# A blocked causal convolution: H1's sums stored in reverse, one F operation for H0, a second output pair split over three engines, and new orders

## The chip, the cores and the metric

One core of one Trainium2 chip. The metric is the device time of one launch in microseconds (us), lower is better.

## The reference

A causal convolution along the sequence with full matrices as taps: each output row is the sum over eight taps of an earlier input row times a 512 x 512 matrix.

```python
B, S, D, K = 8, 4096, 512, 8
out = np.zeros_like(x)                       # x: (B, S, D) float32
for k in range(K):                           # kernel: (K, D, D) float32
    shifted = x moved k rows down, zeros ahead
    out += np.matmul(shifted, kernel[k])
```

## The kernel before

**Tiling.** The 8 x 4096 rows are cut into 128 runs of 256 consecutive rows, one run per partition. A product is a 128 x 512 by 512 x 512 matrix product in bf16 (4 matmuls of 128 x 512, accumulated in PSUM): it applies one matrix to one row position of all 128 runs. The input is loaded with a cast to bf16 into DRAM buffers `xd` (GpSimd's queue), four rows at a time, and transposed from there into `XR`, a ring of 20 row positions (SyncE's queue).

**Fewer products.** The first 4 rows of each run are computed directly (`direct(tap, t)`, 32 products). The other 252 are done in 21 blocks of 12 rows. A block has four nodes, in this order: PL, MI, H1, H0. A node takes sums and differences of input rows and of the eight weight matrices (the weight sums `wsum` and `plus` are made once, on VectorE) and needs 9 products. Nodes 3 and 4, of the first block, are "leaf" nodes: they take 11 products and fewer sums. The outputs are put together from the four nodes' results.

**Names.** `do(name, k)` runs one step of node k; an order is a list of tokens `name.i`, where i counts from the block's PL node (0 PL, 1 MI, 2 H1, 3 H0, 4 and up the next block's). The steps of a node:
- VectorE: `z` (row differences or sums from XR into Z), `s` (sums of Z rows two apart, into S), `A` (two sums of neighbouring Z rows), `F0` and `F1` (two sums each of neighbouring S rows, into F). All are bf16 with both inputs in SBUF. `d0` and `d1` make the first half of a PSUM pair from the second and DT.
- TensorE: `a1`, `a0`, `u` (three products into the bank pair q), `v0`, `v1` (from S), `l00`, `l01`, `l10`, `l11` (from F).
- ScalarE: a copy inside q behind a1; `s0`, `s1` (seeds of the result pairs p[0], p[1]), `dt` (DT).
- `e0`, `e1` take the result pairs out of PSUM: PL's on ScalarE (into cc, two passes), MI's on VectorE (into dd), H1's and H0's on VectorE into y buffers, with a store. H0's writes dd in place.
- `ga0`, `gb0`, `ga1`, `gb1`: the two halves of the middle outputs, cc and dd added on GpSimd, with a store. `E0` (ScalarE copies the second half of H1's first pair) and `ya0` (GpSimd adds dd to it) split H1's first pair.
- `r0`, `r1`, `r2`: GpSimd issues the load of four rows three blocks ahead; `x12`, `x16`, `x20`: SyncE issues a transpose.

In H0 four of the five s rows are computed, the fifth is H1's, which lies in S already; F0 of H0 reads it by a broadcast.

**What sets the order.** The schedule is manual: each engine runs its instructions in the order in which the program emits them, and waits only for the data and the buffers. `ORDER` is run once per block; ahead of it stands a long hand-written start for the first two blocks. S, F, Z and DT exist once, so the next node's step waits until the last reader of the old contents is through. Output tiles come from a pool of 5 buffers (`ypool`), handed out in the order in which they were released. `behind(i)` adds a wait: a GpSimd operation or load starts only after the VectorE operation emitted last. In the last block ga1 has no such wait.

Of the kernel before, what the change touches and what calls it, by code (L numbers as in the profile page):

```python
# [14 lines left out]
def kernel(  # L15
# [244 lines left out]
    def node_e(n, b_):  # L260
        p, t = n.p[b_], n.t + 2 * b_
        first = n.k <= 4
        if n.a == PL:
            cc[b_] = y_tile()
            if first:
                nc.scalar.mul(out=cc[b_], in_=p, mul=0.5)
            else:
                nc.scalar.copy(out=cc[b_], in_=p)  # L268
                dd[b_] = y_tile()
                nc.scalar.mul(out=dd[b_], in_=cc[b_], mul=-0.5)  # L270
        elif n.a == MI:
            if first:
                dd[b_] = y_tile()
                stt(dd[b_], p, -0.5, cc[b_], ADD)
            else:
                stt(dd[b_], p, 0.5, dd[b_], ADD)
        elif n.a == H1:
            yy[b_] = yy.get(b_) or y_tile()
            if first or b_ == HI:
# [4 lines left out]
        elif n.k == len(nodes) - 1 and b_ == HI:
            for j, eng in ((HI, nc.scalar), (LO, nc.sync)):
                stt(dd[b_][:, j], dd[b_][:, j], -1.0, p[:, j], SUB)
                eng.dma_start(out=orr[:, t + 8 + j, :], in_=dd[b_][:, j])
        else:
            if first:
                tt(dd[b_], dd[b_], p, SUB)  # L290
            else:
                stt(dd[b_], dd[b_], -1.0, p, SUB)
# [2 lines left out]
    def node_E(n):
        if n.a == H1 and n.k > 4:
            yy[LO] = yy.get(LO) or y_tile()
            nc.scalar.copy(out=yy[LO][:, 1], in_=n.p[LO][:, 1])

    def node_y(n):  # L300
        if n.a == H1 and n.k > 4:
            y = yy.pop(LO)
            behind(nc.gpsimd.tensor_tensor(out=y[:, 1], in0=y[:, 1], in1=dd[LO][:, 1], op=SUB))
            store(n.t, y)
# [4 lines left out]

    def middle_half(n, b_, j):  # L310
        behind(nc.gpsimd.tensor_tensor(out=cc[b_][:, j], in0=cc[b_][:, j], in1=dd[b_][:, j], op=ADD), b_ > j and n.k)  # L311
# [132 lines left out]
    nc.vector.memset(zero, 0.0)
    nc.sync.dma_start(out=XF, in_=xr[:, 0:4, :])
    cast(nc.vector.tensor_copy, 2, 4)
    make_identity(nc, ident)
    for k in range(7):
        fill(pair(2 + k % 2))
    rows(H[:, 4:8], RUN - 4, 4)  # L450
    cast(nc.scalar.copy, 0, 2)
    transpose_pe("x0", 2, xin[0], 0, 4)
    load_w(0)
    load_w(4)
    fill(pair(3))
    fill(pair(3))
    here(nc.scalar.copy, 0, "x0", 0, 2)
    transpose_pe("h4", 3, H, 4, 8)
    here(nc.scalar.copy, 0, "x0", 2, 4)
    fill(pair(2))  # L460
    history(nc.scalar.copy, -4, "h4")
    direct(0, 1)
    go(3, "v0")
    go(2, "d1")
    direct(0, 0)
    direct(0, 2)
    direct(0, 3)
    direct(4, 2)
    fill(pair(2))
    load_w(1)  # L470
    direct(4, 0)
    direct(1, 1)
    direct(1, 3)
    wsum(MI, HI, HI)
    load_w(5)
    load_w(3)
    wsum(MI, HI, LO)
# [89 lines left out]
    node_a1(nodes[2])
    go(1, "s")
    node_v(nodes[1], 1)
    direct_out(1)  # L570
    go(1, "l01")
    go(1, "l00")
    node_d(nodes[1], 1)
    go(1, "e0")
    go(1, "u")
    go(1, "a0")
    transpose_x(12)
    go(1, "l10")
    go(1, "z")
    do("x16", 1)  # L580
    go(1, "l11")
    go(1, "s1")
    wsum(H1, MID, MID)
    go(1, "s0")
    go(1, "v0")
    go(1, "dt")
    go(1, "F0")
    go(1, "A")
    go(1, "d0")
    go(1, "a1")  # L590
    go(2, "F1")
    go(1, "v1")
    go(2, "l01")
    go(2, "l00")
# [108 lines left out]
```

## Time and profile before

| | |
|---|---|
| time, median of 3 runs | 718.18 us (717.39 to 718.66) |
| the profiled execution | span 717.2 us, 8960 instructions; its device time isn't listed apart from the runs, the lowest of which is 717.39 us |
| TensorE matmuls | 696.0 us busy (97%), 3205 instructions |
| VectorE | 683.3 us (95%), 767 |
| ScalarE | 287.7 us (40%), 448 |
| GpSimd | 167.5 us (23%), 180 |
| granted TensorE clock | 0.998 |
| DMA | 138.86 MB, mean 194 GB/s |

An engine's busy time says nothing of when it was needed: matmuls are pipelined, and the record of one (0.38 us) overlaps the next. Lines of the profile name the line, the engine, the operation, its output and input by the program's names (pp: PSUM pairs, y: output buffers, w: weights, WX and the early S and A), the sizes and a count. VectorE is DVE, ScalarE ACT, GpSimd POOL, SyncE SP. All two-input operations of VectorE are emitted by `tt` (L84) or `stt` (L87), so the output's name and size tell which step a row is. Consecutive rows of the same kind are merged, with their count behind the x.

### The profile page before, as it was taken

The page shows a single profiled execution, that of the slowest core. Times are in us where ns is not written, and L with a number is a line of the kernel's source. Part 1 is how long each engine was busy: PE and PEld are TensorE (multiplying, and loading weights), DVE is VectorE, ACT ScalarE, POOL GpSimd, SP SyncE. Part 2 cuts the span into 40 slices and gives each one's busy share as a digit, 9 for nine tenths or more (in the row PEclk, how much of TensorE's full clock was granted, in tenths as well). Part 3 has the DMA queues.
Part 4 walks back from the last instruction along what each step waited for, and adds up shares of the span by engine and source line. Part 5 has one row for each costly group of instructions (what it writes and reads, how often), then busy time and mean ns, then how long its engine had stood idle before and what let it go on. Part 6 is the DMA issues. An engine that isn't in the chain of part 4 may idle for free.

```text
span 717.2 us, 8960 instructions
## 1 busy us (share of the span) xinstructions
PE 696.0 (97%) x3205; PEld 315.0 (44%) x3270; DVE 683.3 (95%) x767; ACT 287.7 (40%) x448; POOL 167.5 (23%) x180
## 2 busy tenths in 40 slices
PE   7989999999999999999999999999999999999995
PEld 3444444444444444444444444444444444444442
DVE  1899999999999999999999999999999999999994
ACT  3043244343435444343443434353443434444341
POOL 4200012213131221304122131312213041221212
PEclk9999999999999999999999999999999999999999
DMA  9996988788797878879788887977788698855414
GB/s 194 209 225 139 235 156 243 158 233 181 206 226 174 233 167 231 181 189 217 182 241 158 231 184 205 229 176 229 168 237 174 189 224 178 238 119 186 157 68 175
DMA packets 159515, 138.86 MB, mean 194 GB/s; under 512 B 130160, under 2 KB 134256, under 8 KB 159344
## 3 DMA queue, kind: packets, MB, share of 16 engines
q1 hardware_dynamic: 145312, 99.37, 46.6%
q0 software_dynamic: 13728, 38.15, 31.6%
q10 hardware_dynamic: 432, 0.79, 0.3%
q8 instruction: 25, 0.41, 0.2%
q14 instruction: 18, 0.15, 0.1%
HBM read 77.33 MB, written 99.09 MB: 246 GB/s over the span
## 4 chain that ended last, share of the span: by engine, by line
PE 84%; DVE 5%; issue 5%; DMA 0%; POOL 0%; DVEq 0%; POOLq 0%
PE pp L127 84%; DVE w L84 2%; DVE Z L84 2%; DVE y L87 1%; DVE S L84 1%; DMA out_dram<-y 0%; POOL y L311 0%; DVE y L84 0%; DVE F L84 0%; DVE pp L87 0%; DVE pp L84 0%; POOL xd L93 0%; DVEq L84 0%; DVEq L87 0%; POOLq L93 0%
## 5 line engine op out<-in xcount | busy, mean ns | idle before, releaser
L127 PE MATMUL pp<-w,F 128*128 128x512 bf16 x1285 | 310.4, 379 | 3.2 <-DVE pp L87 1.3
L127 PE MATMUL pp<-w,Z 128*128 128x512 bf16 x941 | 231.9, 379 | 2.7 <-DVE Z L84 1.7
L127 PEld LDWEIGHTS <-F 128*128 128x128 bf16 x1312 | 128.3, 98 | 157.6 <-issue 3.4
L311 POOL TENSOR_TENSOR y<-y 128x512 f32<-128x512 f32 x80 | 101.7, 1272 | 406.0 <-DVE F L84 266.1
L127 PE MATMUL pp<-w,S 128*128 128x512 bf16 x658 | 157.5, 379 | 0.7
L84 DVE TENSOR_TENSOR Z<-XR 128x2048 bf16<-128x2048 bf16 (+3 forms) x109 | 154.5, 1435 | 2.5
L127 PEld LDWEIGHTS <-Z 128*128 128x128 bf16 x960 | 92.3, 98 | 118.2 <-DVE Z L84 9.4
L198 ACT COPY pp<-pp 128x512 f32<-128x512 f32 x82 | 46.7, 570 | 221.1 <-PE pp L127 221.1
L84 DVE TENSOR_TENSOR S<-Z 128x2560 bf16<-128x2560 bf16 (+1 forms) x81 | 114.5, 1413 | 0.0
L84 DVE TENSOR_TENSOR F<-S 128x1024 bf16<-128x1024 bf16 x160 | 111.1, 694 | 1.9 <-PE pp L127 1.9
L127 PEld LDWEIGHTS <-S 128*128 128x128 bf16 x672 | 65.8, 98 | 79.4 <-issue 0.2
L214 ACT COPY pp<-pp 128x512 f32<-128x512 f32 (+1 forms) x84 | 48.9, 582 | 76.5 <-PE pp L127 76.5
L93 POOL DMA_DIRECT2D xd<-in_x_dram x61 | 32.7, 536 | 103.7 <-DVE F L84 48.6
L84 DVE TENSOR_TENSOR pp<-DT,pp 128x512 f32<-128x512 f32 x82 | 56.3, 687 | 0.2 <-PE pp L127 0.2
L87 DVE SCALAR_TENSOR_TENSOR pp<-pp,DT 128x512 f32<-128x512 f32 x82 | 56.5, 689 | 0.0
L216 ACT ACTIVATE pp<-pp 128x512 f32<-128x512 f32 (+1 forms) x84 | 50.1, 596 | 15.2 <-PE pp L127 9.8
L84 DVE TENSOR_TENSOR Z<-Z 128x1024 bf16<-128x1024 bf16 x78 | 53.4, 684 | 0.7
L87 DVE SCALAR_TENSOR_TENSOR y<-pp,y 128x1024 f32<-128x1024 f32 x42 | 51.0, 1215 | 0.0
L220 ACT COPY DT<-pp 128x512 f32<-128x512 f32 x82 | 48.9, 597 | 2.6 <-PE pp L127 2.6
L268 ACT COPY y<-pp 128x1024 f32<-128x1024 f32 x40 | 40.6, 1016 | 22.9 <-PE pp L127 21.7
L87 DVE SCALAR_TENSOR_TENSOR y<-y,pp 128x1024 f32<-128x1024 f32 (+1 forms) x41 | 48.3, 1181 | 0.3 <-PE pp L127 0.3
L270 ACT ACTIVATE y<-y 128x1024 f32<-128x1024 f32 x40 | 42.3, 1057 | 2.8 <-DMA out_dram<-y 0.6
(35 smaller groups left out, 248.5 us busy)
## 6 DMA issues: line engine op xcount, KB each, us to landing
out_dram<-y SPq DMA_DIRECT2D x126, 512.0 KB, 4.2
xd<-in_x_dram POOLq DMA_DIRECT2D x61, 512.0 KB, 5.6
w<-in_kernel_dram POOLq DMA_DIRECT2D x8, 512.0 KB, 16.8
w<-in_x_dram SPq DMA_DIRECT2D x1, 1024.0 KB, 4.8
w<-in_x_dram POOLq DMA_DIRECT2D x2, 512.0 KB, 14.0
XR<-xd SPq DMA_TRANSPOSE x61, 4.8
out_dram<-y ACTq DMA_DIRECT2D x3, 256.0 KB, 3.4
w<-in_x_dram POOLq DMA_DIRECT2D x2, 256.0 KB, 18.1
```

The lines of the kernel that those rows point to most:

```text
L84: last["dve"] = nc.vector.tensor_tensor(out=o, in0=a, in1=b, op=op)
L87: last["dve"] = nc.vector.scalar_tensor_tensor(out=o, in0=a, scalar=by, in1=b, op0=MUL, op1=op)
L93: return nc.gpsimd.dma_start(out=o, in_=src)
L127: nc.tensor.matmul(bank, lhsT=comp[:, c * P:(c + 1) * P], rhs=w[:, c, :], start=start and c == 0, stop=c == DC - 1, skip_group_check=True)
L198: nc.scalar.copy(out=n.q[:, 0], in_=n.q[:, 1])
L214: nc.scalar.copy(out=o, in_=q)
L216: nc.scalar.mul(out=o, in_=q, mul=-1.0)
L220: nc.scalar.copy(out=DT, in_=n.q[:, 0])
L268: nc.scalar.copy(out=cc[b_], in_=p)
L270: nc.scalar.mul(out=dd[b_], in_=cc[b_], mul=-0.5)
L311: behind(nc.gpsimd.tensor_tensor(out=cc[b_][:, j], in0=cc[b_][:, j], in1=dd[b_][:, j], op=ADD), b_ > j and n.k)
```

## The change

H1's five s rows are written to S in reverse, so the row that H0 takes over from it is row 0, and H0's four F sums become one operation over rows 0 to 4 (`F.3`). H1's second pair is split like its first: VectorE takes the first half, ScalarE copies the second (`E1`), GpSimd adds dd (`ya1`). The signs and scales of cc and dd change: PL's e is one pass on ScalarE, `m0` and `m1` double cc later, H0's e is a plain subtraction. Tap 0's weights are loaded in four parts (`q0` to `q3`), and its 16 matmuls are issued part by part (`P0` to `P3`). The first cast and the first copies are shared differently between VectorE and ScalarE, the identity is made behind the first loads. ORDER is new, and the start is a token list, `SETUP`, that reaches into the third block.

```diff
-            tt(n.s[:, 0:4], n.z[:, n.o + 1:n.o + 5], n.z[:, n.o + 3:n.o + 7], ADD)
+            tt(n.s[:, 1:5], z[:, o + 1:o + 5], z[:, o + 3:o + 7], ADD)
+        elif n.rev:
+            tt(n.s[:, ::-1], z[:, o:o + 5], z[:, o + 2:o + 7], ADD)
...
-        if not n.shares:
-            tt(f, s[:, 2 * b_:2 * b_ + 2], s[:, 2 * b_ + 1:2 * b_ + 3], ADD)
-        elif b_ == LO:
-            tt(f, s[:, 0:1].to_broadcast([P, 2, D]), s[:, 1:5:3], ADD)
-        else:
-            tt(f, s[:, 1:3], s[:, 2:4], ADD)
+        n.whole = b_ is None
+        a, b = (0, 4) if n.whole else (2 * b_, 2 * b_ + 2)
+        i = 2 - a if n.rev and not n.whole else a
+        tt(F[:, a:b], n.s[:, i:i + b - a], n.s[:, i + 1:i + 1 + b - a], ADD)
...
-            if first:
-                nc.scalar.mul(out=cc[b_], in_=p, mul=0.5)
-            else:
-                nc.scalar.copy(out=cc[b_], in_=p)
-                dd[b_] = y_tile()
-                nc.scalar.mul(out=dd[b_], in_=cc[b_], mul=-0.5)
+            nc.scalar.mul(out=cc[b_], in_=p, mul=0.5)
         elif n.a == MI:
-            if first:
-                dd[b_] = y_tile()
-                stt(dd[b_], p, -0.5, cc[b_], ADD)
-            else:
-                stt(dd[b_], p, 0.5, dd[b_], ADD)
+            dd[b_] = y_tile()
+            stt(dd[b_], p, -0.5, cc[b_], ADD)
         elif n.a == H1:
             yy[b_] = yy.get(b_) or y_tile()
-            if first or b_ == HI:
-                tt(yy[b_], p, dd[b_], ADD if first else SUB)
+            if b_ in SPLIT:
+                tt(yy[b_][:, 0], p[:, 0], dd[b_][:, 0], ADD)
+            else:
+                tt(yy[b_], p, dd[b_], ADD)
                 store(t, yy.pop(b_))
...
+            tt(dd[b_], dd[b_], p, SUB)
             store(t + 8, dd[b_])
...
+    def node_E(n, b_):
+        yy[b_] = yy.get(b_) or y_tile()
+        nc.scalar.copy(out=yy[b_][:, 1], in_=n.p[b_][:, 1])
+
+    def node_y(n, b_):
+        y = yy.pop(b_)
+        behind(nc.gpsimd.tensor_tensor(out=y[:, 1], in0=y[:, 1], in1=dd[b_][:, 1], op=ADD))
+        store(n.t + 2 * b_, y)
+
+    def twice(n, b_):
+        nc.scalar.mul(out=cc[b_], in_=cc[b_], mul=2.0)
...
+    def direct_part(c):
+        w = W[(K - 1) >> 2, (K - 1) >> 1 & 1, (K - 1) & 1]
+        for t in range(HEAD):
+            nc.tensor.matmul(pd[t // 2][:, t % 2], lhsT=XR[:, place(t), c * P:(c + 1) * P], rhs=w[:, c, :],
+                             start=c == 0, stop=c == DC - 1, skip_group_check=True)
...
     ORDER = """
-        d1.1 l01.1 l00.1 s.2 a0.2 x12.0 u.2 l10.1 e1.0 s0.2 e0.1 s1.2 l11.1 v0.2 z.3 F0.2 A.3 F1.2 ga0.2
-        v1.2 x20.1 dt.2 a1.3 d0.2 r0.2 l01.2 e1.1 l00.2 s.3 a0.3 u.3 gb0.2 d1.2 e0.2 l10.2 E0.2 z.4 F0.3
-        r1.2 A.4 l11.2 s1.3 F1.3 s0.3 v0.3 v1.3 ya0.2 r2.2 dt.3 d0.3 a1.4 l01.3 e1.2 l00.3 s.4 gb1.2 a0.4
-        d1.3 e0.3 u.4 l11.3 z.5 s0.4 F0.4 A.5 s1.4 dt.4 ga1.2 v0.4 v1.4 l10.3 d0.4 a1.5 d1.4 l00.4 l01.4
-        a0.5 u.5 e0.4 F1.4 e1.3 s.5 s0.5 l10.4 dt.5 s1.5 z.6 A.6 x16.4 l11.4 F0.5 v0.5 v1.5 a1.6 d0.5 F1.5
+        d1.1 l01.1 l00.1 e1.0 a0.2 u.2 s.2 s0.2 l10.1 l11.1 e0.1 m0.1 v0.2 z.3 s1.2 F0.2 v1.2 dt.2 r0.2
+        ga0.2 A.3 e1.1 d0.2 a1.3 l01.2 x12.0 gb0.2 l00.2 F1.2 x20.1 m1.1 d1.2 a0.3 s.3 u.3 e0.2 z.4 l10.2
+        s0.3 l11.2 E0.2 v0.3 r1.2 A.4 F.3 s1.3 dt.3 ya0.2 a1.4 d0.3 v1.3 l01.3 l00.3 e1.2 a0.4 s.4 gb1.2 u.4
+        d1.3 e0.3 z.5 F0.4 E1.2 dt.4 ya1.2 l11.3 s0.4 r2.2 ga1.2 l10.3 v0.4 A.5 s1.4 v1.4 a1.5 d0.4 l00.4
+        l01.4 d1.4 F1.4 a0.5 e0.4 u.5 e1.3 s.5 z.6 l10.4 dt.5 s0.5 x16.4 F0.5 l11.4 v0.5 A.6 d0.5 s1.5 v1.5
+        a1.6 F1.5
...
+    SETUP = """
+        zero f2 f2 H4 f3 f2 f3 f3 q0 f3 q1 X0 f2 q2 f3 q3 k2 f2 id w4 w1 w5 k0 tx0 f3 th4 cx0a vx0b f3 w3 P0
+        ch4 P1 w7 s211 P2 H3 P3 p311 f2 D42 p310 s210 D40 w6 D11 D10 w2 s212 D41 D13 D53 D12 D43 s120 D33
+        D30 D51 p300 s200 s312 D73 X8 th3 s320 ch3 D31 X4 D63 D50 s020 X9 s021 D32 p301 s121 D21 D70 tx8 D62
+        D20 L16 tx4 L28 D52 s321 cx8a s201 tx9 cx4b L20 s302 cx4a D23 f3 L12 s322 cx9a D71 D60 s220 za.1
+        zb.1 A.1 f2 D61 a1.1 sa.1 D72 u.1 a0.1 out0 D22 B44 s0.1 s1.1 sb.1 F0.1 z.2 v0.1 s221 v1.1 A.2 dt.1
+        out1 s222 a1.2 d0.1 l01.1 F1.1 s.2 l00.1 T12 u.2 e0.1 a0.2 d1.1 s202 B40 s0.2 z.3 l10.1 L32 s022
...
+        gb1.7 d1.8 E1.7 e0.8 u.9 z.10 l11.8 F0.9 dt.9 ya1.7
```

In SETUP, `sabc` and `pabc` are weight sums, `Dkt` is direct(k, t), `wk` loads tap k, `H`, `X`, `L` and `B` load rows, `f` are filler matmuls, `t` and `c` or `v` transposes on TensorE and copies from PSUM; a token with a dot is a step of the node with that number.

More of the change, by code (lines that the diff above doesn't have):

```diff
@@ L136, in __init__ @@
             self.shares = a == H0 and not self.leaf
+            self.rev = a == H1 and not self.leaf
+            self.whole = False
             self.s = WX[:, 0:5] if k <= EARLY and k % 2 else S
@@ L287, in node_e @@
                 eng.dma_start(out=orr[:, t + 8 + j, :], in_=dd[b_][:, j])
         else:
[L289 to L292, printed above, removed]
+            tt(dd[b_], dd[b_], p, SUB)
             store(t + 8, dd[b_])
[L295 to L304, printed above, removed]
@@ L306, in middle @@
-    def middle(n, b_):
-        stt(cc[b_], cc[b_], 2.0, dd[b_], SUB)
-        store(n.t + 4 + 2 * b_, cc[b_])
+    def node_E(n, b_):
[7 more added lines that the diff above has]
+        nc.scalar.mul(out=cc[b_], in_=cc[b_], mul=2.0)
     def middle_half(n, b_, j):
-        behind(nc.gpsimd.tensor_tensor(out=cc[b_][:, j], in0=cc[b_][:, j], in1=dd[b_][:, j], op=ADD), b_ > j and n.k)
+        behind(nc.gpsimd.tensor_tensor(out=cc[b_][:, j], in0=cc[b_][:, j], in1=dd[b_][:, j], op=SUB), b_ > j and n.k)
@@ L438, in do @@
             ACTS[name](nodes[k])
-    def go(k, name):
-        do("a1" if name == "b1" else name, k + AHEAD.get(name, 0))
-    pd = {0: pair(0), 1: pair(1)}
[L444 to L477, printed above, removed]
@@ L567 @@
[L567 to L594, printed above, removed]
@@ L624 @@
-    go(3, "a0")
-    wsum(H1, HI, MID)
-    go(2, "v0")
-    go(3, "F0")
-    do("x20", 1)
-    go(3, "e0")
-    go(3, "s0")
-    go(3, "A")
-    go(3, "l10")
-    go(3, "e1")
-    go(2, "d0")
-    go(4, "l01")
-    go(3, "s1")
-    go(4, "l00")
-    behind(load_x(40))
-    go(4, "b1")
-    go(4, "l10")
-    behind(load_x(44))
-    go(4, "s")
-    go(4, "u")
-    go(4, "e0")
-    go(4, "s1")
-    go(4, "s0")
-    go(4, "l11")
-    go(4, "z")
-    go(4, "F0")
-    go(4, "A")
-    go(4, "a0")
-    go(4, "dt")
@@ L653 @@
-    go(3, "d0")
-    go(4, "e1")
-    go(4, "v0")
-    go(4, "v1")
-    go(4, "a1")
-    go(4, "d0")
-    go(4, "d1")
-    done |= {(name, k) for name in ("ga0", "gb0", "ga1", "gb1", "x12", "x16", "x20")
+    PE_T = {"x0": (2, xin[0], 0, 4), "h4": (3, H, 4, 8), "h3": (2, H, 1, 4), "x4": (3, xin[4], 0, 4),
+            "x8": (2, xin[8], 0, 2), "x9": (2, xin[8], 2, 4)}
+    BITS = (LO, HI, MID)
+    FIRST = {
+        "zero": lambda: nc.vector.memset(zero, 0.0),
+        "X0": lambda: nc.sync.dma_start(out=XF, in_=xr[:, 0:4, :]),
+        "k2": lambda: cast(nc.vector.tensor_copy, 1, 4), "k0": lambda: cast(nc.scalar.copy, 0, 1),
+        "id": lambda: make_identity(nc, ident),
+        "H4": lambda: rows(H[:, 4:8], RUN - 4, 4), "H3": lambda: rows(H[:, 1:4], RUN - 7, 3),
+        "X4": lambda: load_xin(4), "X8": lambda: load_xin(8, 0, 2), "X9": lambda: load_xin(8, 2, 4),
+        "ch4": lambda: history(nc.scalar.copy, -4, "h4"), "ch3": lambda: history(nc.scalar.copy, -7, "h3"),
+    }
@@ new lines, with act @@
+    """.split()
+    def act(token):
+        name, _, k = token.partition(".")
+        if token in FIRST:
+            FIRST[token]()
+        elif k:
+            if name in PARTS:
+                done.add((name[0], int(k)))
+                PARTS[name](nodes[int(k)])
+            else:
+                do(name, int(k))
+        elif name.startswith("out"):
+            direct_out(int(name[3:]))
+        elif name[0] == "f":
+            fill(pair(int(name[1:])))
+        elif name[0] == "w":
+            load_w(int(name[1:]))
+        elif name[0] == "T":
+            transpose_x(int(name[1:]))
+        elif name[0] == "L":
+            load_x(int(name[1:]))
+        elif name[0] == "B":
+            behind(load_x(int(name[1:])))
+        elif name[0] == "t":
+            p = PE_T[name[1:]]
+            transpose_pe(name[1:], *p)
+        elif name[0] == "q":
+            n, c = K - 1, int(name[1:])
+            load(W[n >> 2, n >> 1 & 1, n & 1][:, c:c + 1], kr[:, c:c + 1, 0, :])
+        elif name[0] == "P":
+            direct_part(int(name[1:]))
+        elif name[0] in "cv":
+            t, h = int(name[2:3]), name[3:]
+            lo = 0 if h == "a" else 2
+            src = "x" + str(t)
+            here(nc.scalar.copy if name[0] == "c" else nc.vector.tensor_copy, {0: 0, 4: 4, 8: 8, 9: 10}[t], src, lo, lo + 2)
+        elif name[0] == "D":
+            direct(int(name[1]), int(name[2]))
+        elif name[0] in "sp":
+            a, b_, c_ = (int(i) for i in name[1:])
+            if name[0] == "p":
+                plus((b_, c_))
+            else:
+                wsum(a, b_, c_)
```

161 lines of the change are left out of this document (28 added, 133 removed).

## The prediction

> **What bounds the kernel now.** I read the page first, then the waits of TensorE and VectorE, then one block of twelve rows engine by engine, then the first 55 us and the last 15 us.
>
> ```profile
> span 717.2 us, 8960 instructions
> PE 696.0 (97%) x3205; PEld 315.0 (44%) x3270; DVE 683.3 (95%) x767; ACT 287.7 (40%) x448; POOL 167.5 (23%) x180
> ...
> PE pp L127 <- DVE Z L84: 1.7, 3, 0.7
> PE pp L127 <- DVE pp L87: 1.3, 2, 0.7
> ...
> DVE y L84 <- DMA out_dram<-y: 3.0, 2, 1.6
> ```
>
> TensorE is the bound and VectorE is just behind it. Between start and end, TensorE waits for VectorE only 1.7 + 1.3 = 3.0 us. Nearly all of that follows two waits of VectorE for an output buffer (3.0 us): it has so little spare time that a wait of 1.6 us reaches TensorE. GpSimd is free three quarters of the time, but its operations come behind chosen VectorE operations, so its order matters more than its load.
>
> One block, on TensorE (start, us, then the instruction; a product is 4 matmuls):
>
> ```profile
> 142.22 1.03 PE L127 MATMUL pp<-w,Z 128*128 128x512 bf16 x4
> 143.08 1.89 PE L127 MATMUL pp<-w,F 128*128 128x512 bf16 x8
> ...
> 149.99 1.04 PE L127 MATMUL pp<-w,Z 128*128 128x512 bf16 x4
> ...
> 157.77 1.03 PE L127 MATMUL pp<-w,Z 128*128 128x512 bf16 x4
> ```
>
> These are a1.4, then l01.3 with l00.3, then a1.5 and a1.6. From 142.22 to 157.77 are 18 products: 0.864 us each, so 36 products make a block of 31.1 us. The same block on VectorE and GpSimd:
>
> ```profile
> 141.25 0.68 DVE L84 TENSOR_TENSOR F<-S 128x1024 bf16<-128x1024 bf16 x1
> ...
> 143.58 1.48 DVE L84 TENSOR_TENSOR S<-Z 128x2560 bf16<-128x2560 bf16 x1
> 144.98 0.69 DVE L87 SCALAR_TENSOR_TENSOR pp<-pp,DT 128x512 f32<-128x512 f32 x1
> 145.58 1.21 DVE L87 SCALAR_TENSOR_TENSOR y<-y,pp 128x1024 f32<-128x1024 f32 x1
> 146.71 2.02 DVE L84 TENSOR_TENSOR Z<-XR 128x3584 bf16<-128x3584 bf16 x1
> 148.64 0.68 DVE L84 TENSOR_TENSOR F<-S 128x1024 bf16<-128x1024 bf16 x1
> 149.25 0.68 DVE L84 TENSOR_TENSOR Z<-Z 128x1024 bf16<-128x1024 bf16 x1
> ...
> 151.05 0.78 DVE L84 TENSOR_TENSOR F<-S 128x1024 bf16<-128x1024 bf16 x1
> 151.75 1.21 DVE L87 SCALAR_TENSOR_TENSOR y<-y,pp 128x1024 f32<-128x1024 f32 x1
> 152.88 1.48 DVE L84 TENSOR_TENSOR S<-Z 128x2560 bf16<-128x2560 bf16 x1
> 154.29 2.08 DVE L84 TENSOR_TENSOR Z<-XR 128x1536 bf16<-128x1536 bf16 x2
> 156.40 0.69 DVE L84 TENSOR_TENSOR Z<-Z 128x1024 bf16<-128x1024 bf16 x1
> ```
> ```profile
> 142.15 1.27 POOL L303 TENSOR_TENSOR y<-y 128x512 f32<-128x512 f32 x1 [0.59 <-issue]
> 143.37 0.54 POOL L93 DMA_DIRECT2D xd<-in_x_dram  x1
> ...
> 150.01 1.27 POOL L311 TENSOR_TENSOR y<-y 128x512 f32<-128x512 f32 x1 [3.59 <-DVE Z L84]
> ```
>
> VectorE's rows are F1.3, s.4, d1.3, e0.3, z.5, F0.4, A.5, F1.4, e1.3, s.5, z.6, A.6. Start to start, an operation costs: s 1.40, d 0.60, a whole e 1.13, z 1.93 (about 2.0 in two pieces), F and A 0.60. GpSimd: ya0.2, r2.2, ga1.2. A GpSimd sum takes 1.27 and lets the next begin after 1.22, a load's issue takes 0.54. Three latencies follow: A.5 ends at 149.93 and a1.5 starts at 149.99 (0.06); A.5's end to ga1.2, which is behind it, 0.08; F1.3's end at 141.93 to ya0.2, which also needs ScalarE's copy, 0.22.
>
> **The change part by part**
>
> ```profile
> L84 DVE TENSOR_TENSOR S<-Z 128x2048 bf16<-128x2048 bf16 x20 | 24.2, 1212 | 0.0
> ...
> L84 DVE TENSOR_TENSOR y<-pp,y 128x512 f32<-128x512 f32 x20 | 13.6, 678 | 0.0
> ```
>
> *VectorE's load.* e1.2 becomes a half: 0.68 long, 0.60 from start to start, against 1.13. F.3 as one operation over 2048 elements goes by the S row of that size: 1.21 long, about 1.13 start to start, against two F at 1.20. That is 0.6 us per block. By itself it gains nothing, because TensorE sets the 31.1 us; it only absorbs waits. S written in reverse keeps each row of 512 contiguous; I take 1.40, and if it ran at half the speed (about 2.7), H1's s would run into the 0.6 us that VectorE then waits for l00.1 ahead of e0.1, so little would reach TensorE.
>
> *ScalarE and PL's scaling.* e.0 loses its second pass, m adds one, E1 adds a copy; ScalarE is 40% busy and each is ahead of its user. *stt to tt* in e.3 costs nothing (same rows of 1.21).
>
> *The 3.0 us of TensorE waits.* y buffers are handed out in order of release. e1.2's buffer comes from gb0.2's store, and gb0.2 moves ahead of s.3, so one more long VectorE operation lies between it and e1.2; and VectorE has slack now. I take −3.0 (bounds 0 and −3.0).
>
> *The start.*
>
> ```profile
> 1.46 0.72 POOL L93 DMA_DIRECT2D w<-in_x_dram  x1
> ...
> 14.87 1.23 DVE L84 TENSOR_TENSOR w<-w,w 128x2048 bf16<-128x2048 bf16 x1 [1.77 <-DMA w<-in_kernel_dram]
> 19.95 4.63 DVE L84 TENSOR_TENSOR w<-w,w 128x2048 bf16<-128x2048 bf16 x4 [3.86 <-DMA w<-in_kernel_dram]
> ...
> 42.02 1.48 DVE L84 TENSOR_TENSOR Z<-XR 128x2560 bf16<-128x2560 bf16 x1
> ...
> 53.09 1.89 PE L127 MATMUL pp<-w,F 128*128 128x512 bf16 x7 [0.43 <-DVE pp L84]
> ```
>
> VectorE, not the weights' arrival, sets 42.02 and 53.09: both kernels put the same 19 weight sums ahead of node 1's z, and the same 38 products ahead of l01.1. The change moves one sum (p311) into the 3.86 us of idle ahead of 19.95: −1.14 (a start-to-start of the four in 4.63). Between z.1 and l01.1 it has one F less: −0.60. The identity's two operations go behind the first five issues, so the first load goes out up to 0.7 earlier than 1.46; I take half, −0.4, since the loads that follow are one stream. Tap 0 in four parts lets TensorE do 16 matmuls while the rest arrives, but TensorE waits for VectorE at 44 to 53 us anyway: 0; its three extra issues on GpSimd's queue (0.7 each) lie ahead of loads that wait in that stream. Sum −2.1, bounds 0 and −3.
>
> *The end.*
>
> ```profile
> 704.36 1.89 PE L127 MATMUL pp<-w,S 128*128 128x512 bf16 x8
> 706.24 3.62 PE L127 MATMUL pp<-w,F 128*128 128x512 bf16 x15
> ...
> 704.56 0.69 DVE L84 TENSOR_TENSOR F<-S 128x1024 bf16<-128x1024 bf16 x1 [1.93 <-PE pp L127]
> 705.50 0.70 DVE L84 TENSOR_TENSOR pp<-DT,pp 128x512 f32<-128x512 f32 x1 [0.24 <-PE pp L127]
> ...
> 708.24 2.42 DVE L87 SCALAR_TENSOR_TENSOR y<-y,pp 128x1024 f32<-128x1024 f32 x3 [0.31 <-PE pp L127]
> ...
> 707.40 2.51 POOL L311 TENSOR_TENSOR y<-y 128x512 f32<-128x512 f32 x2 [0.65 <-DVE y L84]
> ...
> 710.69 0.33 SPq L287 DMA_DIRECT2D out_dram<-y  x1
> ```
>
> Call l11.2's end x (704.36; F1.3 starts 0.20 later, when TensorE has read F; d0.3 starts 0.28 after v0.3's end). VectorE ends at 710.66, x + 6.30. In the change F.3 (1.13) delays l01.3 by 0.2, and e0.3 starts at about x + 4.1 and ends at x + 5.3. In the last block ya1.2 is behind e0.3, so it starts at x + 5.4 and ga1.2, behind it in GpSimd's queue, ends at x + 7.9. The last half of e1.3 must wait for that: it ends at x + 8.6. +2.3, bounds 0 and +3.
>
> *The new wait in each block: ya1.2, r2.2, ga1.2 and then e1.3.* e1.3 overwrites dd[1], which ya1.2 and ga1.2 read. In the change all three GpSimd operations are behind F0.4, and VectorE has only A.5, d0.4, d1.4 and F1.4 between F0.4 and e1.3. In the clock of the block above, at TensorE's pace:
> - v1.3 now takes the slot 142.22 to 143.08, behind a1.4. s.4 overwrites the S that v1.3 reads, so it starts at 143.28 (0.20 as for F). Then d1.3 144.68, e0.3 145.28, z.5 146.41, F0.4 148.34, ending at 149.02. VectorE cannot be earlier.
> - ya1.2 also needs ScalarE's copy: 149.02 + 0.22 = 149.24. r2.2 at 150.46, ga1.2 at 151.00, ending at 152.27. e1.3 at 152.34.
> - Then s.5 at 153.47, z.6 154.87, F0.5 156.80, A.6 157.40, ending at 158.09; a1.6 can start at 158.15. It is due at 157.77.
>
> So TensorE loses 0.4 us in every block in which r2.2 is there. Loads run three blocks ahead of 21, so these are blocks 1 to 17: 17 × 0.4 = 6.8. Without r2.2's 0.54 the chain just fits. After the loss everything shifts together and nothing else is late; behind e1.3 on VectorE stand s.5, z.6, F0.5 and A.6, and a1.6 waits for the last.
>
> A GpSimd sum that is released while VectorE runs an operation with two SBUF inputs does not occur in this trace. The nearest row is the reverse: F1.4 at 151.05 starts 0.23 before ga1.2 ends at 151.28 and takes 0.78, not 0.68: 0.10 of 0.23 lost, or 0.43. Here ya1.2 arrives with 0.38 of A.5 left, and ga1.2 with some 0.41 of F1.4 left (v1.4 ends at 149.99, so d1.4 starts at 150.27 and F1.4 at 150.87). The low end is no loss, 0.4 a block; the high end is that GpSimd waits for both to the end, 0.97 a block. I take the row's share, 0.43 × 0.79 = 0.34: 0.74 a block, 12.6 over 17, and 0.2 each in blocks 18 and 19, where the chain is 0.54 shorter: +13.0.
>
> **Sum.** −3.0 − 2.1 + 2.3 + 13.0 = +10.2. The profiled execution has a span of 717.2, and the three times run from 717.39 to 718.66; on the median, 718.2, this gives 728.4, and I say 728.
>
> **The rivals**
> - *GpSimd and VectorE shut each other out wholly.* ya1.2 starts at A.5's end (149.62), ga1.2 at F1.4's end (151.55), e1.3 at 152.90: 0.97 a block, or 16.5, and 0.6 each in blocks 18 and 19: 718.2 − 2.8 + 17.7 = 733. For it: F1.4's 0.78 is also what waiting for GpSimd's last read would give. Against: no row shows GpSimd held back. The Trainium skill, SBUF — State Buffer, section Who interferes with whom, states just this: a VectorE operation with two SBUF inputs and a GpSimd operation that reads SBUF take the shared port in turn, and the second waits out the whole of the first. By that rule the time is this rival's; the one row here agrees with it and doesn't prove it.
> - *The chain doesn't bite* (the other side: faster). If GpSimd releases dd[1] by 151.9, a1.6 is on time: that takes 0.4 us less, for example r2.2's issue not holding GpSimd, or VectorE reaching F0.4 earlier. Then the time is 718.2 − 2.8 = 715.4. For it: the margin is one load's issue. Against: every link stands in rows that repeat in each block.
> - *Gains lost:* the output-buffer waits stay and the start gives nothing, and the chain costs little: 718 to 720.
>
> **How the numbers follow.** No run tells less than 0.2% (1.4 us) from no change. Chain with part of the blocking, 728 (own range 722 to 731): 0.40. Whole blocking, 733: 0.22. Chain doesn't bite, 715.4: 0.28. Gains lost: 0.10. Faster is the third case and a little of the fourth, 0.29; same 0.07; slower 0.64. The range takes both outer cases with about 1 us: 714 to 734.
>
> **What would show it.** VectorE's e1.3 with idle time ahead of it put down to GpSimd (about 0.8 to 1.4 us, some 17 times), TensorE's Z products waiting for VectorE's A some 17 times, a block of 31.5 to 32.1 us; ya1.2 starting at A.5's end rather than 0.22 behind F0.4; the first F product near 51 us; the last VectorE operation about 8.6 us behind l11.2's end. The prediction is wrong if the block is still 31.1 us: then the chain's arithmetic failed, and the time is near 715.

## The result and the profile after

The changed kernel takes 739.65 us (median of 5 runs, 737.38 to 741.89) against 718.18 us for the kernel before (median of 5, 717.39 to 719.15): ratio 1.0301, 95% interval 1.0283 to 1.0318. The prediction said 728 with a range of 714 to 734. The direction was right, the size was not, and the time lies above the range. The profiled execution took 737.38 us with a span of 735.6, 18.4 more than before's 717.2. Where a run below fell into a slower state (one of run e1, 737.35 us, one of run e9, 831.93 us, and one of the kernel before, 1268.73 us), it is left out of the times and ratios.

The page of the changed kernel (span, and busy us, share and instructions of each engine), then three rows of its waits (engine, line, released by: us in total, times, longest):

```profile
span 735.6 us, 9045 instructions
PE 699.0 (95%) x3209; PEld 314.5 (43%) x3274; DVE 681.1 (93%) x746; ACT 299.3 (41%) x471; POOL 221.3 (30%) x209
...
DVE y L84 <- POOL y L300: 23.4, 21, 1.2
...
PE pp L127 <- DVE Z L84: 17.5, 22, 1.0
...
DVE y L84 <- POOL y L293: 2.3, 2, 1.5
```

VectorE is less busy than before (681.1 against 683.3), as its shorter steps should make it. But it now waits 23.4 us for GpSimd's sum at L300 (`ga`), about 1.1 us each time, and TensorE waits 17.5 us for VectorE's Z, where the wait before was 1.7. The waits for an output buffer (DMA out_dram, 3.0 us before) are gone.

One block, VectorE's rows s.4 and e0.3 and those from F0.4 on (start, length, instruction, in brackets idle time and releaser), then GpSimd's and TensorE's:

```profile
305.44 1.64 DVE L84 TENSOR_TENSOR S<-Z 128x2560 bf16<-128x2560 bf16 x1
...
307.61 1.21 DVE L84 TENSOR_TENSOR y<-y,pp 128x1024 f32<-128x1024 f32 x1
...
310.67 0.68 DVE L84 TENSOR_TENSOR F<-S 128x1024 bf16<-128x1024 bf16 x1
311.27 0.68 DVE L84 TENSOR_TENSOR Z<-Z 128x1024 bf16<-128x1024 bf16 x1
...
313.07 0.68 DVE L84 TENSOR_TENSOR F<-S 128x1024 bf16<-128x1024 bf16 x1
314.91 1.22 DVE L84 TENSOR_TENSOR y<-y,pp 128x1024 f32<-128x1024 f32 x1 [1.16 <-POOL y L300]
316.05 1.48 DVE L84 TENSOR_TENSOR S<-Z 128x2560 bf16<-128x2560 bf16 x1
...
320.05 0.68 DVE L84 TENSOR_TENSOR Z<-Z 128x1024 bf16<-128x1024 bf16 x1
```
```profile
304.46 1.27 POOL L293 TENSOR_TENSOR y<-y 128x512 f32<-128x512 f32 x1 [1.16 <-DVE F L84]
307.16 1.27 POOL L300 TENSOR_TENSOR y<-y 128x512 f32<-128x512 f32 x1 [1.43 <-DVE S L84]
311.48 1.59 POOL L293 TENSOR_TENSOR y<-y 128x512 f32<-128x512 f32 x1 [3.05 <-issue]
313.03 0.54 POOL L93 DMA_DIRECT2D xd<-in_x_dram  x1
313.57 1.30 POOL L300 TENSOR_TENSOR y<-y 128x512 f32<-128x512 f32 x1
```
```profile
320.79 1.04 PE L127 MATMUL pp<-w,Z 128*128 128x512 bf16 x4 [0.98 <-DVE Z L84]
```

GpSimd's last three rows are ya1.2, r2.2 and ga1.2. ya1.2 has a record of 1.59 us where the same operation elsewhere takes 1.27, and it ends at 313.07. Counted back, its 1.27 us began at 311.80, when VectorE's A.5 (311.27, 0.68) was nearly through: it was held until then. e1.3 (314.91) waits 1.16 us for ga1.2 to end at 314.87, s.5 to A.6 follow, and a1.6 at 320.79 comes 1.0 us late. The row at 307.16 shows the opposite: gb1.2 runs beside d1.3 and e0.3, which have a PSUM operand, and takes its plain 1.27. The row at 304.46, ya0.2, shows the exclusion the other way round: it ends at 305.73, s.4 starts beside it at 305.44 and takes 1.64 us instead of 1.48. So in each of the 19 blocks F0.4 comes 0.16 us later too.

To see where the 18.4 us lie, I mark the same three products in both traces: l01.1, the a1.6 of the first repeated block and that of the last. Two of the rows of before, then those of the changed kernel:

```profile
126.68 1.03 PE L127 MATMUL pp<-w,Z 128*128 128x512 bf16 x4
...
690.55 1.03 PE L127 MATMUL pp<-w,Z 128*128 128x512 bf16 x4
```
```profile
51.28 1.89 PE L127 MATMUL pp<-w,F 128*128 128x512 bf16 x8 [0.39 <-DVE pp L84]
...
128.03 1.04 PE L127 MATMUL pp<-w,Z 128*128 128x512 bf16 x4 [0.97 <-DVE Z L84]
...
706.61 1.04 PE L127 MATMUL pp<-w,Z 128*128 128x512 bf16 x4 [0.89 <-DVE Z L84]
...
720.44 1.67 PE L127 MATMUL pp<-w,S 128*128 128x512 bf16 x7
722.52 3.61 PE L127 MATMUL pp<-w,F 128*128 128x512 bf16 x16 [0.41 <-DVE pp L84]
```

| stretch | before | after | difference |
|---|---|---|---|
| to l01.1 | 53.09 | 51.28 | −1.8 |
| l01.1 to the first a1.6 | 73.6 | 76.8 | +3.2, of which 1.1 is the new stall of a1.6 |
| first to last a1.6, 18 blocks | 563.9 (31.3 each) | 578.6 (32.1 each) | +14.7 |
| last a1.6 to x (l11.2's end) | 13.8 | 13.8 | 0 |
| x to VectorE's last end | 6.3 | 8.7 | +2.4 |

The rest of the span behind VectorE's last end is 0.1 shorter. TensorE's matmuls follow each other every 0.216 us; by that pitch there is a gap of 0.92 to 1.13 us ahead of a1.6 in each of the 19 blocks. Against 36 products of 0.864 us (31.1) the 18 blocks lose 1.04 us each, with the first gap 19.8 us together; in the kernel before the same 18 blocks lose 4.0.

The end in the changed kernel, on VectorE:

```profile
727.25 0.69 DVE L84 TENSOR_TENSOR y<-y,pp 128x512 f32<-128x512 f32 x1 [1.52 <-POOL y L293]
728.48 0.69 DVE L84 TENSOR_TENSOR y<-y,pp 128x512 f32<-128x512 f32 x1 [0.53 <-POOL y L300]
```

The two halves of the last e1.3 wait for ya1.2 and then for ga1.2, as forecast; VectorE ends at 729.17, x + 8.73 (forecast x + 8.6).

### The profile page after: what moved, and what is told of

Same layout as the page of the kernel before. It is cut to its first block, busy times and chain, and to the rows that moved or that the text cites. A ratio compares the mean times of both kernels' runs of the same rounds, so it can differ in the third digit from the quotient of the medians.

```text
span 735.6 us, 9045 instructions
## 1 busy us (share of the span) xinstructions
PE 699.0 (95%) x3209; PEld 314.5 (43%) x3274; DVE 681.1 (93%) x746; ACT 299.3 (41%) x471; POOL 221.3 (30%) x209
## 5 line engine op out<-in xcount | busy, mean ns | idle before, releaser
L127 PE MATMUL pp<-w,F 128*128 128x512 bf16 x1285 | 307.2, 379 | 3.2 <-DVE pp L84 1.7
L127 PE MATMUL pp<-w,Z 128*128 128x512 bf16 x943 | 232.2, 379 | 18.4 <-DVE Z L84 17.5
L127 PE MATMUL pp<-w,S 128*128 128x512 bf16 x657 | 159.9, 379 | 0.6
L300 POOL TENSOR_TENSOR y<-y 128x512 f32<-128x512 f32 x84 | 118.3, 1409 | 86.6 <-ACT y L297 46.9
L84 DVE TENSOR_TENSOR S<-Z 128x2560 bf16<-128x2560 bf16 (+1 forms) x81 | 126.9, 1567 | 0.0
L84 DVE TENSOR_TENSOR F<-S 128x1024 bf16<-128x1024 bf16 (+1 forms) x140 | 106.3, 760 | 2.3 <-PE pp L127 2.3
L293 POOL TENSOR_TENSOR y<-y 128x512 f32<-128x512 f32 x42 | 60.1, 1431 | 104.0 <-issue 60.4
L84 DVE TENSOR_TENSOR y<-y,pp 128x1024 f32<-128x1024 f32 (+1 forms) x43 | 51.1, 1189 | 25.7 <-POOL y L300 23.4
L268 ACT ACTIVATE y<-pp 128x1024 f32<-128x1024 f32 x42 | 43.1, 1027 | 25.0 <-POOL y L300 13.0
L87 DVE SCALAR_TENSOR_TENSOR y<-pp,y 128x1024 f32<-128x1024 f32 x42 | 51.2, 1219 | 0.0
```

What stands on the lines that cost most here:

```text
L84: last["dve"] = nc.vector.tensor_tensor(out=o, in0=a, in1=b, op=op)
L87: last["dve"] = nc.vector.scalar_tensor_tensor(out=o, in0=a, scalar=by, in1=b, op0=MUL, op1=op)
L127: nc.tensor.matmul(bank, lhsT=comp[:, c * P:(c + 1) * P], rhs=w[:, c, :], start=start and c == 0, stop=c == DC - 1, skip_group_check=True)
```

## The experiments

Theory A: e1.3 writes dd[1], which ya1.2 and ga1.2 must have read; and GpSimd's sums and a VectorE operation with both inputs in SBUF shut each other out wholly. Rivals: the two overlap in part (the prediction's own chain), the extra load on GpSimd slows VectorE's rows everywhere, or the new order as such costs the time. In the ratios below the kernel before ran beside each (717.5 to 718.3 us).

The runs are called run e1 to run e11; e0.3 or e1.3, with a point, are steps of a node.

**Which term of the chain counts: r2.2 behind ga1.2 (run e3), and all three behind A.5 (run e4)**

```diff
-  s0.4 r2.2 ga1.2 l10.3
+  s0.4 ga1.2 r2.2 l10.3
```

> The changed kernel, but the load r2.2 is issued behind ga1.2 instead of ahead of it, 17 blocks. Theory A (whole exclusion): ga1.2 could start 0.5 us earlier, but F1.4 then holds it back until its own end, so ga1.2 ends where it ended, and the time stays within 2 us of the changed kernel's. The prediction's own chain (partial sharing): 0.3 to 0.5 us less per block, 5 to 9 us less.

738.73 us against the changed kernel's 739.65, ratio to before 1.0299 (1.0281 to 1.0316). The same block in this kernel, GpSimd, then VectorE's F1.4:

```profile
311.18 1.59 POOL L293 TENSOR_TENSOR y<-y 128x512 f32<-128x512 f32 x1 [3.05 <-issue]
312.74 1.83 POOL L300 TENSOR_TENSOR y<-y 128x512 f32<-128x512 f32 x1
314.51 0.54 POOL L93 DMA_DIRECT2D xd<-in_x_dram  x1
```
```profile
312.77 0.68 DVE L84 TENSOR_TENSOR F<-S 128x1024 bf16<-128x1024 bf16 x1
```

ga1.2 starts without the 0.54 us of the load ahead of it, and its record grows from 1.30 to 1.83, by just that. F1.4 goes first, although its record starts 0.03 us after that of ga1.2, and ga1.2 ends where it would have: 1.12 us behind F1.4's end in both kernels. My 0.54 us of r2.2, on which the prediction let the whole chain turn, is worth nothing that shows. This also explains blocks 18 and 19, which have no r2.2 and stall the same 1.0 us.

```diff
-  dt.4 ya1.2 l11.3 s0.4 r2.2 ga1.2 l10.3 v0.4 A.5 s1.4
+  dt.4 l11.3 s0.4 l10.3 v0.4 A.5 ya1.2 r2.2 ga1.2 s1.4
```

> The changed kernel, but ya1.2, r2.2 and ga1.2 are released by A.5 instead of F0.4, one VectorE operation later. Theory A (whole exclusion: ya1.2 already waits for A.5 to end): only the latency of the new wait, 0 to 0.15 us per block, 0 to 3 us more, and ya1.2's record shrinks from 1.59 to 1.27. Partial sharing (ya1.2 runs beside A.5 and loses 0.43 of 0.38 us): 0.3 us per block, 5 to 6 us more. No exclusion at all: 0.46 us per block, 9 us more.

741.92 us, ratio 1.0347 (1.0328 to 1.0367): 2.3 above the changed kernel by the medians, 4.4 by the two profiled executions. The time lies between the two theories and doesn't decide. The rows do (GpSimd, and the group of L293 in each kernel: count, busy us and mean ns; the changed kernel first):

```profile
L293 POOL TENSOR_TENSOR y<-y 128x512 f32<-128x512 f32 x42 | 60.1, 1431 | 104.0 <-issue 60.4 <-DVE F L84 42.0 <-ACT y L289 1.5
```
```profile
312.91 1.27 POOL L293 TENSOR_TENSOR y<-y 128x512 f32<-128x512 f32 x1 [3.65 <-issue]
...
L293 POOL TENSOR_TENSOR y<-y 128x512 f32<-128x512 f32 x42 | 54.5, 1297 | 114.2 <-issue 71.2 <-DVE F L84 41.4 <-ACT y L289 1.5
```

Released by A.5 (in this trace 312.10 to 312.78), ya1.2 takes 1.27. It starts 0.13 after the end of A.5's record, while in the changed kernel its work began 0.15 before that end: the new release costs 0.28 us, not the 0 to 0.15 that I gave it, and 0.28 in 19 blocks is 5.3. (The blocks take 32.4 us here, 32.1 in the changed kernel.)

**The wait itself: a buffer of its own for e1.3 (run e1)**

```diff
-            tt(dd[b_], dd[b_], p, SUB)
-            store(t + 8, dd[b_])
+            y = y_tile() if b_ == HI and n.k > 4 else dd[b_]
+            tt(y, dd[b_], p, SUB)
+            store(t + 8, y)
```

> The changed kernel, but from the second block on H0's second output pair (e1.3) goes to an output buffer of its own instead of over dd[1]; only the last block keeps the old form. All GpSimd work stays, and so does whatever it does to VectorE's rows. Theory A (e1.3 must wait until ya1.2 and ga1.2 have read dd[1], and GpSimd and VectorE shut each other out wholly while both read two inputs from SBUF, so that this chain ends 1.04 us late in each of 19 blocks): e1.3 follows F1.4 at once, the waits of the Z products for A.6 go, 17 to 19 us less: 721 to 724. Rival B (the cost is the load itself: VectorE's rows stretched beside GpSimd's 42 more sums, s.3 1.70 against 1.21): 737 to 740. Rival C (with one more user the five output buffers run short): the 19 waits go, but VectorE waits for stores instead: 727 to 740.

725.11 us (719.63 to 727.66), ratio 1.0097 (1.0068 to 1.0127), profiled at 724.85: 12.5 us less than the profiled changed kernel. All the GpSimd work is still there (219.1 us busy against 221.3). From the groups by form and from the waits of this kernel:

```profile
L127 PE MATMUL pp<-w,Z 128*128 128x512 bf16 x943 | 232.2, 379 | 6.7 <-DVE Z L84 5.6
...
L84 DVE TENSOR_TENSOR S<-Z 128x2048 bf16<-128x2048 bf16 x20 | 33.4, 1669 | 0.0
...
DVE Z L84 <- DMA XR<-xd: 11.8, 13, 2.9
```

VectorE's wait for `ga` falls from 23.4 us to 1.4, and TensorE's wait for Z from 17.5 to 5.6. s.3 is still stretched (1669 ns, 1212 before), and the shortest blocks take 31.1 us all the same, so the stretching is not what costs the 19.8 us: rival B falls. (The GpSimd sums are 126 against 100 before, 26 more and not 42.) No row of VectorE waiting for an output buffer is left, so rival C falls too. What is left is another wait that I hadn't named: z waits 11.8 us for transposed rows. So the time is 1 to 4 us above what I gave theory A.

**Without the third GpSimd sum (run e2)**

```diff
-            if b_ in SPLIT:
+            if b_ == LO or n.k < 9:
...
-  F0.4 E1.2 dt.4 ya1.2 l11.3
+  F0.4 dt.4 l11.3
```

> The changed kernel, but H1's second pair is taken whole by VectorE again from node 11 on (no E1.2, no ya1.2; r2.2 and ga1.2 stay behind F0.4). The start is left as it is. Theory A: ga1.2 can start at A.5's end and is through before e1.3 is due, the waits of 1.04 us go, and with ya1.2 out of the last block the end is 1.3 to 2.4 us shorter too: 717 to 720. Rival D (the other new orders cost, not the third GpSimd sum): 730 or more.

724.11 us, ratio 1.0092 (1.0077 to 1.0107). The 1.0 us stall is gone from every block but the first, which the unchanged start feeds, but the time stays 4 us above my range. The end is 2.2 us shorter than in the changed kernel, within the 1.3 to 2.4 that I gave, but still 0.2 longer than in the kernel before (VectorE ends at x + 6.5, there at x + 6.3). A block takes 31.5 us. VectorE is the bound in this kernel, busy almost without a break through the block; its two stretched rows, and the GpSimd rows beside them:

```profile
279.08 0.97 DVE L84 TENSOR_TENSOR F<-S 128x1024 bf16<-128x1024 bf16 x1
...
295.44 1.69 DVE L84 TENSOR_TENSOR S<-Z 128x2048 bf16<-128x2048 bf16 x1
```
```profile
278.20 1.28 POOL L300 TENSOR_TENSOR y<-y 128x512 f32<-128x512 f32 x1
...
294.40 1.65 POOL L300 TENSOR_TENSOR y<-y 128x512 f32<-128x512 f32 x1 [0.28 <-DVE pp L84]
```

F1.4 (0.68 alone) starts at 279.08 while ga1.2 runs to 279.48 and is 0.29 longer. gb0.2 at 294.40 meets F1.2 and is 0.38 longer; s.3 then meets gb0.2 and is 0.48 longer. Here it is VectorE that waits.

**Taking the two stretches away (runs e5, e6, e7)**

```diff
e5, on e2:   l01.2 x12.0 [gb0.2 out] l00.2 F1.2 x20.1 m1.1 [d1.2 out] a0.3 s.3 [gb0.2 in] u.3 [d1.2 in] e0.2
e6, on e2:   s0.4 ga1.2 r2.2 l10.3
e7:          both, and E1 and ya1 out of SETUP too
```

> The kernel of e2_whole_pair (H1's second pair whole on VectorE, 724.1), with gb0.2 released by s.3 instead of by d0.2, and d1.2 moved behind s.3, so that gb0.2 runs beside d1.2 and e0.2, which read PSUM. In e2_whole_pair a block took about 31.5 us with VectorE busy all through it, s.3 at 1.69 (1.21 alone) and F1.4 at 0.97 (0.68 alone). Theory A (whole exclusion also holds VectorE back, 0.48 and 0.28 a block, and this is what e2_whole_pair still loses): s.3 goes back to 1.21, 0.3 to 0.46 us less per block, 5 to 8 us in all: 716 to 719. Rival D (the new order itself, whatever runs on GpSimd): 723 to 725.

722.68 us, ratio 1.0065 (1.0043 to 1.0088): 1.4 us less than run e2, not 5 to 8, and the two intervals overlap. s.3 is back at 1225 ns. The 0.48 us was there to save, but the blocks went only from 31.5 to 31.4 us: VectorE now idles 0.1 us ahead of s.3 and F1.4 is still held.

> The kernel of e2_whole_pair, with r2.2 issued behind ga1.2 instead of ahead of it: ga1.2 then starts at A.5's end and runs beside d0.4 and d1.4, and is through when F1.4 starts. Theory A: F1.4 goes from 0.97 to about 0.75 and 0.2 us less per block in 17 blocks, 3 to 4 us: 720 to 721. If F1.4's longer record were not on the path: 724.

721.60 us, ratio 1.0049 (1.0030 to 1.0069): 2.5 us less, somewhat under the forecast 3 to 4; F of 1024 elements is back at 684 ns in the mean.

> Both of these edits together, and in the start too H1's second pair is taken whole by VectorE (no E1 or ya1 at all). Theory A: nothing holds VectorE back any more, TensorE sets 31.1 us per block again, the start is 1.8 us and the end 1.5 us shorter than before: 713 to 717, faster than the kernel before by 0.2 to 0.6%. Rival D: 722 or more.

722.99 us, ratio 1.0064 (1.0038 to 1.0089), with runs from 718.79 to 728.49 (the profiled one, 725.83, is among the slower). Not faster. The stretches are gone (s.3 1225, F 683 ns), but an old wait is back, from this kernel's waits:

```profile
DVE y L84 <- DMA out_dram<-y: 8.1, 4, 3.9
PE pp L127 <- DVE pp L87: 5.1, 3, 3.1
```

gb0.2 now comes behind s.3 as in the kernel before, its store later, and e1.2 waits for the buffer. The place alone isn't the cause: run e5 has it too, and no such wait. In the four blocks in which e1.2 waits here, gb0.2's store took 5.0 to 7.0 us to land, in the others 4.2 at most, in run e5 3.6 at most. The two waits of the kernel before are of the same kind (5.8 and 5.7 us, else 4.1 at most). So the place sets how much lateness e1.2 can bear; why some stores land late, no run here shows.

**gb0.2 early, in the kernel before alone (run e10)**

```diff
-  a1.3 d0.2 r0.2 l01.2 e1.1 l00.2 s.3 a0.3 u.3 gb0.2 d1.2 e0.2
+  a1.3 d0.2 gb0.2 r0.2 l01.2 e1.1 l00.2 s.3 a0.3 u.3 d1.2 e0.2
```

> The kernel before, with gb0.2 alone moved: released by d0.2, ahead of r0.2, instead of by s.3. The prediction's step: this frees e1.2's buffer earlier and takes the 3.0 us of output-buffer waits away; GpSimd's sum then partly overlaps s.3, at most 0.5 us of VectorE per block by theory A, which has little to spare. Waits gone and s.3 not stretched: 715. Waits gone and s.3 stretched by 0.3 to 0.5: 717 to 722. Waits stay: 718.

729.33 us, ratio 1.0155 (1.0142 to 1.0168). The output-buffer waits are gone altogether: there is no such row among this kernel's waits. But ga0.2 and gb0.2 run back to back into s.3 (the group, then the rows of one block):

```profile
L84 DVE TENSOR_TENSOR S<-Z 128x2048 bf16<-128x2048 bf16 x20 | 42.5, 2125 | 0.0
...
294.86 2.16 DVE L84 TENSOR_TENSOR S<-Z 128x2048 bf16<-128x2048 bf16 x1
```
```profile
293.44 2.50 POOL L311 TENSOR_TENSOR y<-y 128x512 f32<-128x512 f32 x2 [14.04 <-DVE F L84]
```

s.3 starts at 294.86, GpSimd ends at 295.94, and s.3 takes 0.95 us more than its 1.21: nearly all of the overlap. I had allowed 0.5 at most. Over 20 blocks the mean of 2125 is 18 us of VectorE, of which 11 reach the time. One move takes a 3 us wait away and costs 14.

**Both kept apart (run e9, then run e11)**

> H1's second pair whole on VectorE everywhere and r2.2 behind ga1.2, as in e7_both, but gb0.2 early: e1.1 is moved behind F1.2 and d0.2, gb0.2 is released by d0.2 and then runs beside e1.1 and d1.2 (PSUM readers) instead of beside F1.2 and s.3. In e7_both VectorE's rows were back at their own lengths, but e1.2 waited 8.1 us for an output buffer, which gb0.2's store gives back, and this reached TensorE. Theory A (whole exclusion, and the place of gb0.2 decides when e1.2's buffer is free): neither wait is left, about 31.1 us per block, start and end shorter than before: 713 to 717. If e1.2's wait for a buffer has another cause: 720 or more.

```diff
on e2, with e7's r2.2 and SETUP:
-  ga0.2 A.3 e1.1 d0.2 a1.3 l01.2 x12.0 gb0.2 l00.2 F1.2 x20.1 m1.1 d1.2 a0.3 s.3
+  ga0.2 A.3 F1.2 d0.2 gb0.2 a1.3 l01.2 x12.0 e1.1 l00.2 x20.1 m1.1 d1.2 a0.3 s.3
```

821.88 us, ratio 1.1473 (1.1435 to 1.1511). Here is z.4 in one block, and SyncE's queue; then the sum over the run, from the waits:

```profile
290.94 2.02 DVE L84 TENSOR_TENSOR Z<-XR 128x3584 bf16<-128x3584 bf16 x1 [4.08 <-DMA XR<-xd]
```
```profile
284.87 0.34 SPq L257 DMA_DIRECT2D out_dram<-y  x1
285.30 5.32 SPq L100 DMA_TRANSPOSE XR<-xd  x2
```
```profile
DVE Z L84 <- DMA XR<-xd: 81.3, 19, 5.3
```

This was a slip of mine: with gb0.2 I moved its store ahead of the transpose x12.0 in SyncE's queue. The store waits for GpSimd's sum, so x12.0 and x20.1 go out one after the other from 285.30 on, and z.4 has its rows at 290.9. The wait is not the whole cost. In the same block TensorE stops, and for a while behind the stop its matmuls are slower:

```profile
293.74 1.89 PE L127 MATMUL pp<-w,Z 128*128 128x512 bf16 x4 [3.38 <-DVE Z L84]
...
297.13 3.07 PE L127 MATMUL pp<-w,F 128*128 128x512 bf16 x8
...
301.76 1.89 PE L127 MATMUL pp<-w,F 128*128 128x512 bf16 x8
```

Behind 15 of the 18 stops (3.6 to 5.0 us from one matmul's start to the next's) the next 7 to 13 matmuls start 0.43 us apart, not 0.22. The granted clock is 0.55 from 292 to 299 us, and 0.952 over the run. TensorE's waits for VectorE's Z come to 70.0 us and the slower matmuls to about 29, together nearly all of the 102 us by which the span (818.0) exceeds that of the next run (715.6).

```diff
-  d0.2 gb0.2 a1.3 l01.2 x12.0 e1.1
+  d0.2 x12.0 gb0.2 a1.3 l01.2 e1.1
```

> As e9_order, but the transpose x12.0 is issued ahead of gb0.2 again. In e9_order gb0.2's store stood ahead of x12.0 in SyncE's queue, so the transpose was held until GpSimd's sum was through, and z.4 waited 81 us in all for its rows. With x12.0 ahead of that store these waits go (0 to 3 us left, as in the changed kernel); gb0.2 is early and runs beside e1.1 and d1.2, so neither a buffer wait nor a stretched s.3 is left: 713 to 717. If z.4 still waits, or VectorE lacks the time for the later d0.2: 719 to 725.

718.64 us, ratio 1.0024 (1.0006 to 1.0042), profiled at 717.38 with a span of 715.6. One token's place is worth 103 us. Neither a stretched s.3 (1212 ns) nor a buffer wait is left, and TensorE's wait for VectorE's Z is 0.3 us in all. It is the best of the variants, 21 us below the changed kernel, yet no faster than the kernel before; the forecast of 713 to 717 failed. The end gives nothing (x + 6.5; the 1.5 us that I had promised myself there, in run e7 too, was misread). Between l01.1 and the first a1.6 it loses 2.7 us in TensorE's gaps, against 1.0 in the kernel before. And its runs scatter from 716.62 to 723.18, most of them above the profiled one; by what, no profile here shows.

**F.3 alone, in the kernel before (run e8)**

```diff
+        elif n.rev:
+            tt(n.s[:, ::-1], n.z[:, n.o:n.o + 5], n.z[:, n.o + 2:n.o + 7], ADD)
...
+            if b_ == HI:
+                tt(F, n.s[:, 0:4], n.s[:, 1:5], ADD)
+            return
```

> The kernel before, with one part of the change alone: H1 stores its s rows in reverse and H0's four F sums are one operation, at the place where F1.3 stood. Prediction's step: s in reverse at full speed, 1.48; VectorE 0.07 us shorter per block, nothing gained by itself, up to 1.5 us through the waits that it absorbs: 716 to 718. If writing in reverse cost half the speed: s of H1 at 2.7 us, 720 to 740.

719.36 us, ratio 1.0021 (1.0012 to 1.0030). S of 2560 elements, reversed ones among them, has a mean of 1480 ns (1479 before): writing in reverse costs nothing. F.3 takes 1218 ns. The time is 1.2 us more, not less; the profile shows no cause for it that I could name (its buffer waits are 2.5 us, about as before).

## Why the prediction was wrong

- *The new wait.* Its mechanism was right: e1.3 waits for ya1.2 and ga1.2 (23.4 us in all), A.6 and a1.6 come late, at just these places, and run e1 removes nearly all of it by removing the wait alone. **Its size was the step that failed.** I took 0.34 us of blocking per block, 43% of the overlap, from one row in which F1.4 lost 0.10 of 0.23, and so 0.74 us in 17 blocks and 0.2 in two: 13.0. Measured are 1.04 us in 19 blocks, 19.8. The two engines exclude each other wholly, and at one place more than the chain had: ya0.2 holds s.4 back by 0.16 us. The rival with that rule said 0.97 a block, close to the 1.04, but its 0.6 for blocks 18 and 19 was wrong too: under exclusion r2.2's 0.54 us lies inside the time in which F1.4 holds ga1.2 (run e3).
- The row that I used was read wrongly, as a share. In run e10 the records overlap by 1.08 and VectorE loses 0.95; at gb0.2 and s.3 in run e2 by 0.61, and s.3 loses 0.48. Both times 0.13 us are left over, as if the port were free again that long before the record ends. F1.4's 0.10 of 0.23 in the kernel before is the same: 0.23 less 0.13. So the loss is the overlap less a constant, and a share taken from a short overlap is mostly that constant. The kernel before already had rows against a share: here gb0.2 ends at 138.21, z.4 starts 0.11 us earlier and takes 2.02 us, as it does alone; 43% of the overlap would have added 0.05.

```profile
136.94 1.27 POOL L311 TENSOR_TENSOR y<-y 128x512 f32<-128x512 f32 x1 [0.96 <-DVE S L84]
```
```profile
138.10 2.02 DVE L84 TENSOR_TENSOR Z<-XR 128x3584 bf16<-128x3584 bf16 x1
```

- By the Trainium skill, SBUF — State Buffer, section Who interferes with whom, the second of the two is blocked for the whole operation of the first. The traces agree, but for those last 0.13 us: ya1.2's record of 1.59 against 1.27, ga1.2's 1.83, s.3's 2.16 against 1.21. I had given that rule 0.22 because no row of before showed GpSimd held back; it deserved more.
- *The start:* −2.1 forecast, −1.8 measured, in part by luck. Up to l01.1 the kernel before, run e8 and run e10 have the same start and take 53.09, 52.22 and 51.98 us; the changed kernel and runs e1 to e4 share the new one and take 50.95 to 51.85. So the gain is about 1.0, somewhere between 0.1 and 2.1. *The end:* +2.3 forecast, +2.4 measured, with the mechanism as described. *The buffer waits:* −3.0 forecast, gone; run e10 shows that gb0.2's place does it, as I said. In the 18 blocks TensorE lost 4.0 us before, 3.3 of them beside the two waits; nothing of that is left. What I left out is its price: the same move puts gb0.2 beside F1.2 and s.3, 0.48 us of VectorE a block. Where VectorE has only half of e1.2 to do it bears this (run e1 has it and blocks of 31.1 us); in run e2, with e1.2 whole, it shows.
- *Not in the sum:* between l01.1 and the first a1.6 the changed kernel loses 2.0 us more than the one before, besides the new stall: TensorE's gaps over 84 products come to 3.0 us (the largest 0.9), against 1.0 (the largest 0.5). In runs e7 and e11 they are still 2.3 and 2.7, and these have no E1 or ya1 in the start, so SETUP's order is a part of it; which part I did not separate.
- *S in reverse, F.3, the plain subtraction:* at full speed, as forecast (1480, 1218 and 1219 ns or less where nothing holds them).
- The sum by terms: −1.8 + 2.4 + 19.8 − 4.0 + 2.0 = 18.4, by which the spans differ. The medians differ by 21.5. The changed kernel's median is 2.3 us above its profiled execution. By the 1.8 us between that execution's time and span, before's profiled execution would have taken 719.0 (an estimate), 0.8 above its median. These 3.1, the 2.0 and the 2.1 by which the stalls exceed its 17.7 are most of why even the rival's 733 falls short; why the runs of the changed kernel spread over 4.5 us, and those of before over 1.8, stays open.

## What to carry to other kernels

Before work goes to an idle GpSimd, look at what VectorE runs beside it: with both of VectorE's inputs in SBUF the two take turns, whoever comes second waits nearly to the end, and the idle share of GpSimd says nothing of it. Place such sums beside VectorE operations that read PSUM, and count the whole of each neighbour into any chain that ends in a wait for GpSimd. When a step is moved, follow its DMA in its queue too: a store that waits for data holds every transfer behind it.
